# Placing every long SBUF row of an fp32 transformer kernel at a multiple of 512 bytes

## The chip, the cores and the metric

The kernel runs on one core of one Trainium2 chip. The metric is the device time of one execution in microseconds; the time quoted is the median of three runs.

## The reference

Two small models run one after the other on 256 tokens of 1,024 features, all in fp32. Block 1: a gated MLP mixer over 128-token blocks, a gated feed-forward layer with a causal convolution of width 3, attention over 64-token chunks with a relative bias, a second such feed-forward layer, and a norm. Block 2: a mixer that joins stick-breaking attention with a delta-rule recurrence, a feed-forward layer with a per-layer embedding gated in, latent attention with rotated keys, a second such layer, and the last norm. The products are the bulk of it; each has this form, `h` being 256 x K and `w` K x N:

```python
def conv_ffn(h, w_in, conv_w, conv_b, w_down):
    a = h @ w_in
    ...
    up, gate = jnp.split(a, 2, axis=-1)
    return (jax.nn.silu(gate) * up) @ w_down
```

## The kernel before

**The products.** Every weight matrix is cut into tiles of 128 x 128 and packed in the order of use, eight tiles to a chunk (`CT`), 399 chunks in all. `Net._chunk` (lines 392 to 406) loads a chunk of 128 x 1,024 fp32 into `raw` on SP's queue, ScalarE rounds it into a high part `whi` (line 404), and VectorE subtracts to get the low part `wlo` (line 405); both are of the type fp32r. Two chunks are prepared ahead of their use. The activations lie feature-major, 128 features by 256 tokens, and are cut the same way into `xh` and `xl` (`split`, lines 477 to 482). `gemm_tile` (lines 425 to 432) then makes three matmuls for each weight tile, each with a weight load of 128 columns and a moving operand of 256 columns:

```python
            self.mm(ps, wh, xh, start=first and k == 0, stop=False)
            self.mm(ps, wh, xl, start=False, stop=False)
            self.mm(ps, wl, xh, start=False, stop=k == n - 1)
```

`gemm_rows` (lines 450 to 460) turns the roles round for the attention values: the activations are the stationary operand and four weight tiles, 512 columns, move.

**The order.** In each phase TensorE takes its instructions as a list written by hand gives them (`GMLP_ORDER`, `ATT_ORDER`, `HYB_ORDER`, `MLA_ORDER`; `gated_layer`, lines 785 to 827, for the feed-forward layers). In `ffn1` (lines 829 to 869, the first block) both halves of the hidden row go through the convolution, in `ffn2` (lines 905 to 947) one does. Each has 22 hidden tiles, with 48 matmuls for the two halves of one (the up product), and then a product down of 8 output tiles with 66 matmuls each.

**The memory.** Each partition's SBUF is filled from both ends. From the low end, in `Net.__init__` (lines 328 to 334), come pools that live throughout: `cp` (gains and constants), `hp` (the residual rows `h`), `raw`, `whp`, `wlp`, `sp` (small and short tiles) and `xp` (operand tiles). The phases take turns at the two ends of what remains (`phase`, lines 463 to 469): a phase's pool holds its tiles, long and short ones mixed. A pool places each tag's buffers behind the last, in steps of 32 bytes. The kernel's first tile begins at byte 16,512; the gains (704 columns) and the first constants (258 columns) follow, so that `h` begins at byte 20,384, which is 416 past a multiple of 512. What lies behind keeps that offset until a short tile shifts it:

| tiles | begin, past a multiple of 512 | past a multiple of 64 |
|---|---|---|
| `h`, `raw`, `whi`, `wlo` | 416 | 32 |
| `xh`, `xl` of `xp`: most products | 224 | 32 |
| `xh`, `xl` of the mixer's and the attention's own pool | 480, 96 | 32 |
| `f1` tiles of the hybrid mixer, its last product | 288 | 32 |
| `hh`, `hl` (down products), `xh`, `xl` of the embedding's gate | 320 | 0 |
| `xh`, `xl` of the latent attention's own pool | 64 | 0 |

Every row of a tile, or of the slice that an instruction takes, is a multiple of 512 bytes here, so that the offset of a tile is that of all its slices: a weight tile's row is 512 bytes, a moving operand's 1,024 or 2,048.

**Short chains.** `newton` (lines 497 to 517) makes 1/sqrt for columns of 2, 4, 8 or 16 values per partition with eleven VectorE instructions, in tiles of that width.

Of the kernel before, what the change touches and what calls it, by code (L numbers as in the profile page):

```python
# [10 lines left out]
F32 = mybir.dt.float32  # L11
F32R = mybir.dt.float32r
I32 = mybir.dt.int32
# [7 lines left out]
P = 128  # L21
# [5 lines left out]
CT = 8           # 128x128 weight tiles in one chunk  # L27
HT = 2           # feature tiles of h in one load
LOOK = 2         # chunks prepared ahead of their use
# [5 lines left out]
# ---------------------------------------------------------------- layout tables  # L35
# per-feature vectors, one column of 128 values per feature tile
# [22 lines left out]
def _shape_consts():  # L59
    """Constants that depend on the shapes alone."""  # L60
# [28 lines left out]
    # rope: rows of a head's tile; even heads [64 plain | 32 cos | 32 sin], odd heads [32 sin | 32 cos | 64 plain]  # L89
# [24 lines left out]
# where, in steps of a gated layer's first product, what does not belong to it goes  # L114
# [40 lines left out]
class Sums:  # L155
    """sums of squares per token, gathered tile by tile"""
# [18 lines left out]
    def mean(self, dim):  # L175
        """mean of squares + eps, [128 tokens, 2]"""
        net = self.net
        ps = net.pa([P, 2])
        self.total(ps)
        x = net.t(net.sp, [P, 2], "msq")  # L180
        net.nc.vector.tensor_scalar(x, ps, 1.0 / dim, EPS, ALU.mult, ALU.add)
        return x


class Norm:
    """rms norm of h, gains applied: parts X of the unscaled rows at once, their scales in two later steps"""
# [22 lines left out]
class Last:  # L209
    """norm(h) * g of the last rows, gathered tile by tile, and its way out"""  # L210
# [15 lines left out]
    def total(self, n):  # L226
        """add up to n tiles"""
# [7 lines left out]
    def write(self):  # L235
# [5 lines left out]
        # 1/sqrt(x): square root and reciprocal, and a Newton step  # L241
        y, z, w, r = (net.t(net.sp, [P, 2], f"nwy2_{k}") for k in (0, 1, 2, 0))
# [17 lines left out]
class Hidden:  # L260
    """parts of a gated layer's hidden rows, each in three steps"""
# [25 lines left out]
class Embed:  # L287
    """half of norm(p @ w) * g, feature-major, in steps that go between the tiles of a longer product"""
# [31 lines left out]
class Net:  # L320
    def __init__(self, ctx, tc, d, nchunks):
# [5 lines left out]
        pool = lambda name, bufs, **k: ctx.enter_context(tc.tile_pool(name=name, bufs=bufs, **k))  # L327
        self.cp = pool("cp", 1)
        self.hp = pool("hp", 1)
# [16 lines left out]
    # ------------------------------------------------------------ small helpers  # L346
# [4 lines left out]
    def t(self, pool, shape, tag, dt=F32, **k):  # L351
        return pool.tile(shape, dt, tag=tag, name=self.uid(tag), **k)
# [20 lines left out]
    def load_consts(self, pool, group):  # L373
        w = sum(CONSTS[n].shape[1] for n in CGROUP[group])
        ct = self.t(pool, [P, w], "cst_" + group, bufs=1)
# [15 lines left out]
    # ------------------------------------------------------------ weights  # L391
# [16 lines left out]
    def after(self, ins):  # L408
        """VectorE issues this after the last chain of short operations"""
        if self.fence is not None:  # L410
            self.tc.add_manual_dep(ins.ins, self.fence.ins.name, NOSYNC, reason="order")

    def w(self, name, idx, k0, cols, n=1):
        """the next n 128x128 weight tiles, as (high, low) parts of [128, 128 n]"""
# [19 lines left out]
    def gemm_pair(self, X, ps, name, idx, parts, late=False, mid=None, at=0):  # L434
        """two output tiles in one bank; late: the last input tile comes last for both; mid: call within the second"""
# [10 lines left out]
    def pe_order(self):  # L446
        """TensorE takes its instructions as they are written down"""
        return self.tc.manual_schedule(engines={E.PE})

    def gemm_rows(self, X, ps2, name, idx, c0, ks=None, n=None, cols=lambda c0, j: ((c0 + j * P, P),)):  # L450
        """token-major: ps2[t] = tokens of block t by 512 columns"""
# [10 lines left out]
    # ------------------------------------------------------------ splits and norms  # L462
    @contextmanager
    def phase(self, name, xbufs=1):
        """a pool of its own for a phase; the phases take turns at the two ends of the free memory"""
        self.side ^= 1
        with self.tc.tile_pool(name=name, bufs=2, side="right" if self.side else "left", reuse_waits="tile") as p:
# [3 lines left out]
    def xtile(self, own=True):  # L471
        """high and low part of one operand tile, out of the phase's pool or of the one that all phases share"""
# [4 lines left out]
    def split(self, h, gain, own=True):  # L477
        """high and low parts of h * gain"""
# [18 lines left out]
    def newton(self, x, n, out=None, alone=False):  # L497
        """1/sqrt(x), x [128, n]"""
        v, sp = self.nc.vector, self.sp
        i = self.t(sp, [P, n], f"nwi{n}", I32)  # L500
        j = self.t(sp, [P, n], f"nwj{n}", I32)
# [3 lines left out]
        a = self.t(sp, [P, n], f"nwa{n}")  # L505
        b = self.t(sp, [P, n], f"nwb{n}")
        ys = [self.t(sp, [P, n], f"nwy{n}_{k}") for k in range(3)]
# [11 lines left out]
    def stats(self, tiles, dim):  # L519
        """rT [128 tokens, 2] = 1/rms, and the same along the free axis in every partition, [128, 256]"""  # L520
# [14 lines left out]
    def bcast(self, rT=None, dg=None):  # L535
        """[128 tokens, 2] -> along the free axis in every partition, [128, 256]"""
# [10 lines left out]
    def proj_residual(self, X, name, idx, tiles=range(KD), late=False):  # L547
        """late: the first two tiles take the last input tile at their ends"""
# [11 lines left out]
    # ------------------------------------------------------------ start  # L560
# [14 lines left out]
    # ------------------------------------------------------------ block 1  # L575
    def gmlp(self):
# [4 lines left out]
        with self.phase("gmlp", 8) as p:  # L581
# [49 lines left out]
            def mix(q):  # L631
                """two groups' values mixed over the tokens"""
# [20 lines left out]
    def out_steps(self, X, name, idx):  # L653
        """the steps of a product into h, each output tile in two, the second one for the last input tiles"""
# [12 lines left out]
    def steps(self, order, env):  # L667
        """a phase as a list of steps, name.argument.argument, in the order in which TensorE takes them"""
# [1042 lines left out]
```

## Time and profile before

| | |
|---|---|
| median of three runs | 1331.22 us (1328.53 to 1332.67) |
| profiled execution, span from first to last instruction | 1329.0 us |
| TensorE matmuls busy | 1302.5 us, 98% |
| weight loads busy | 1241.6 us, 93% |
| VectorE busy | 1026.6 us, 77% |
| ScalarE busy | 781.1 us, 59% |
| GpSimd busy | 15.7 us, 1% |
| TensorE's granted clock, mean of the span | 0.986 |

The profiled execution's own time is not listed apart from its span; the span lies 2.2 us under the median and inside the range of the three runs. Busy matmul time counts a matmul from its start to a modelled end, and neighbours overlap, so 98% says that TensorE always has a matmul under way, not that it runs at its best: for that one looks at the distance from one matmul's start to the next one's, the pitch.

### The profile page before, as it was taken

Reading aid. Unit: us, or ns where it says so; the run is one execution under the profiler, and the core shown is the slowest. Engines: PE = TensorE matmul, PEld = TensorE weight load, DVE = VectorE, ACT = ScalarE, POOL = GpSimd, SP = SyncE. Lnnn points to the kernel's source line nnn. Section 1 sums busy time; section 2 is a strip of 40 time slices with the busy share of each in tenths; the row PEclk is TensorE's granted clock in tenths of the full one; section 3 lists DMA queues with packets and bytes.
Section 4 is the critical chain, followed back from the end, with each engine's and each line's share of the span. In section 5 each row is a group of like instructions: output and inputs, shape, how many; then the busy total and the mean of one; then the engine's idle time right before and its main releaser. Section 6 shows DMA issues by size and latency. Waiting matters only on the chain.

```text
span 1329.0 us, 27117 instructions
## 1 busy us (share of the span) xinstructions
PE 1302.5 (98%) x10864; PEld 1241.6 (93%) x10864; DVE 1026.6 (77%) x2037; ACT 781.1 (59%) x1359; POOL 15.7 (1%) x48
## 2 busy tenths in 40 slices
PE   7999999999999999999999999999999999999997
PEld 5999999988899999999876799999998999999996
DVE  5889997666679997568964488887779978889655
ACT  6666665457667665448443265655556776565444
POOL 0000000000000000001100000000000000000000
PEclk9999999999999999999998799999999999999998
DMA  7565555555445555564440055555554335555551
GB/s 268 165 232 188 185 186 188 190 180 178 134 144 191 190 186 185 186 236 143 126 126 17 33 180 189 188 179 190 188 176 163 110 126 185 189 190 178 189 191 48
DMA packets 70397, 223.17 MB, mean 168 GB/s; under 512 B 13408, under 2 KB 15712, under 8 KB 70272
## 3 DMA queue, kind: packets, MB, share of 16 engines
q1 hardware_dynamic: 63312, 212.43, 47.9%
q10 hardware_dynamic: 6192, 5.34, 1.4%
q0 software_dynamic: 768, 3.67, 0.8%
q8 instruction: 85, 1.39, 0.4%
q14 instruction: 40, 0.33, 0.1%
HBM read 218.53 MB, written 2.88 MB: 167 GB/s over the span
## 4 chain that ended last, share of the span: by engine, by line
PE 94%; DVE 3%; DMA 1%; ACT 1%; issue 0%; SPq 0%; DVEq 0%; ACTq 0%
PE g L371 80%; PE s L371 6%; PE t L371 4%; PE o L371 3%; PE t L768 1%; DVE wlo L405 1%; DMA raw<-in_wall 1%; DMA b<-dZ 0%; DVE tm L1202 0%; DMA b<-dY 0%; DVE tm L1204 0%; DVE xl L481 0%; DMA dY<-tm 0%; DVE sqa L167 0%; ACT whi L404 0%
## 5 line engine op out<-in xcount | busy, mean ns | idle before, releaser
L371 PE MATMUL g<-xh,whi 128*128 128x256 f32 x2184 | 619.7, 284 | 1.4 <-ACT xh L480 1.4
L404 ACT ACTIVATE whi<-raw 128x1024 fp32r<-128x1024 f32 (+1 forms) x400 | 421.7, 1055 | 331.4 <-PE g L371 174.9
L405 DVE TENSOR_TENSOR wlo<-raw,whi 128x1024 fp32r<-128x1024 f32 (+1 forms) x400 | 487.4, 1220 | 166.8 <-ACT whi L404 165.6
L371 PE MATMUL g<-xl,whi 128*128 128x256 f32 x2184 | 611.6, 280 | 1.8 <-DVE xl L481 1.8
L371 PE MATMUL g<-xh,wlo 128*128 128x256 f32 x2184 | 610.5, 280 | 0.1
L371 PEld LDWEIGHTS g<-xh,whi 128*128 128x128 f32 x2184 | 411.3, 188 | 7.2 <-issue 4.0
L371 PEld LDWEIGHTS g<-xl,whi 128*128 128x128 f32 x2184 | 410.6, 188 | 3.1 <-DVE xl L481 2.4
L371 PEld LDWEIGHTS g<-xh,wlo 128*128 128x128 f32 x2184 | 410.5, 188 | 0.3 <-DVE wlo L405 0.3
L371 PE MATMUL g<-hl,whi 128*128 128x256 f32 x704 | 196.9, 280 | 0.0
L371 PE MATMUL g<-hh,whi 128*128 128x256 f32 x704 | 196.9, 280 | 0.0
L371 PE MATMUL g<-hh,wlo 128*128 128x256 f32 x704 | 196.9, 280 | 0.0
L371 PEld LDWEIGHTS g<-hh,wlo 128*128 128x128 f32 x704 | 132.3, 188 | 0.0
L371 PEld LDWEIGHTS g<-hh,whi 128*128 128x128 f32 x704 | 132.3, 188 | 0.0
L371 PEld LDWEIGHTS g<-hl,whi 128*128 128x128 f32 x704 | 132.3, 188 | 0.0
L273 ACT ACTIVATE hh<-pr 128x256 fp32r<-128x256 f32 x88 | 36.0, 409 | 49.4 <-DVE pr L268 49.4
L852 ACT ACTIVATE c<-pad,vec 128x256 f32<-128x256 f32 x88 | 47.7, 589 | 9.3 <-DVE pad L841 9.3
L480 ACT ACTIVATE xh<-h,vec 128x256 fp32r<-128x256 f32 x80 | 39.0, 498 | 23.9 <-DVE h L545 20.8
L859 DVE SCALAR_TENSOR_TENSOR c<-pad,vec,c 128x256 f32<-128x256 f32 x88 | 42.7, 485 | 3.1
L481 DVE SCALAR_TENSOR_TENSOR xl<-h,vec,xh 128x256 fp32r<-128x256 f32 x80 | 37.7, 478 | 6.8 <-ACT xh L480 6.8
L857 DVE SCALAR_TENSOR_TENSOR c<-pad,vec,c 128x256 f32<-128x256 f32 x88 | 42.1, 478 | 0.0
L278 DVE TENSOR_TENSOR hl<-pr,hh 128x256 fp32r<-128x256 f32 x88 | 36.8, 418 | 3.9 <-ACT hh L273 3.9
L371 PE MATMUL g<-whi,xh 128*128 128x512 f32 x68 | 29.4, 432 | 9.4 <-ACT xh L480 9.4
(375 smaller groups left out, 1392.8 us busy)
## 6 DMA issues: line engine op xcount, KB each, us to landing
raw<-in_wall SPq DMA_DIRECT2D x398, 512.0 KB, 3.5
bias<-in_bias POOLq DMA_DIRECT2D x4, 768.0 KB, 6.7
cst_c<-in_c ACTq DMA_DIRECT2D x1, 896.0 KB, 7.0
raw<-in_wall SPq DMA_DIRECT2D x2, 256.0 KB, 4.2
h<-in_x ACTq DMA_DIRECT2D x2, 256.0 KB, 4.4
h<-in_x POOLq DMA_DIRECT2D x2, 256.0 KB, 7.5
ws<-in_ws ACTq DMA_DIRECT2D x1, 512.0 KB, 8.5
bs<-in_bs ACTq DMA_DIRECT2D x1, 512.0 KB, 8.4
```

Of the source, the lines that this page charges most:

```text
L273: self.net.nc.scalar.activation(self.H[-1][0], self.pr, AF.Copy)
L278: self.net.nc.vector.tensor_tensor(hl, self.pr, hh.bitcast(F32), ALU.subtract)
L371: self.nc.tensor.matmul(out, lhsT=lhsT, rhs=rhs, start=start, stop=stop, skip_group_check=True)
L404: nc.scalar.activation(hi[:, s], raw[:, s], AF.Copy)
L405: self.after(nc.vector.tensor_tensor(lo[:, s], raw[:, s], hi[:, s].bitcast(F32), ALU.subtract))
L480: self.nc.scalar.activation(xh, h, AF.Copy, scale=gain)
L481: self.nc.vector.scalar_tensor_tensor(xl, h, gain, xh.bitcast(F32), ALU.mult, ALU.subtract)
L768: self.nc.tensor.transpose(pt[:, b * P:b * P + P], w[:, s * P:s * P + P], self.cst["ident"])
L852: a.activation(c0, pad[:, j, 2:], AF.Identity, bias=self.col("f_conv_b", (l,), j * KF + i), scale=cw(2, j))
L857: v.scalar_tensor_tensor(c1, pad[:, j, 1:S + 1], cw(1, j), cc[n], ALU.mult, ALU.add)
L859: v.scalar_tensor_tensor(cc[n], pad[:, j, 0:S], cw(0, j), c1, ALU.mult, ALU.add)
```

## The change

Comments are dropped, and these edits are made:

- Two tiles that nothing uses are placed, 672 bytes at the low end behind `cp` and a new pool `sp_odd`, and 480 bytes at the high end. With them `h` begins at byte 22,528 (44 x 512), and the tiles at the high end are placed down from byte 228,864 (447 x 512).
- `Net.t` sends a tile of `sp` or of a phase whose row isn't a whole multiple of 128 elements to a second pool (`sp_odd`, or the phase's name with `_odd`), opened inside the phase's own.
- Constants loaded for a phase get a tile rounded up to 128 columns.
- `newton` for 2, 4 and 8 columns uses tiles of 8 columns under one set of tags, of which it takes the first `n`; the last norm's `write` does the same.

No instruction's operation, shape or order in the source is changed. The core of the diff:

```diff
+ROW = 128
+LEFT_GAP, RIGHT_GAP = 672, 480
...
         self.cp = pool("cp", 1)
+        self.odd = {"sp": pool("sp_odd", 2)}
+        for side, n in (("left", LEFT_GAP), ("right", RIGHT_GAP)):
+            pool("gap_" + side, 1, side=side).tile([P, n // 4], F32, tag="gap", name=self.uid("gap"))
         self.hp = pool("hp", 1)
...
     def t(self, pool, shape, tag, dt=F32, **k):
+        if math.prod(shape[1:]) % ROW:
+            pool = self.odd.get(pool.name, pool)
         return pool.tile(shape, dt, tag=tag, name=self.uid(tag), **k)
...
-        ct = self.t(pool, [P, w], "cst_" + group, bufs=1)
+        ct = self.t(pool, [P, w if pool is self.cp else -(-w // ROW) * ROW], "cst_" + group, bufs=1)[:, 0:w]
...
         self.side ^= 1
-        with self.tc.tile_pool(name=name, bufs=2, side="right" if self.side else "left", reuse_waits="tile") as p:
+        pool = lambda n: self.tc.tile_pool(name=n, bufs=2, side="right" if self.side else "left", reuse_waits="tile")
+        with pool(name) as p, pool(name + "_odd") as odd:
+            self.odd[name] = odd
             self.p, self.xbufs = p, xbufs
             yield p
...
-        i = self.t(sp, [P, n], f"nwi{n}", I32)
-        j = self.t(sp, [P, n], f"nwj{n}", I32)
+        new = lambda tag, dt=F32: self.t(sp, [P, max(n, 8)], f"nw{tag}{max(n, 8)}", dt)[:, 0:n]
+        i, j = new("i", I32), new("j", I32)
...
-        a = self.t(sp, [P, n], f"nwa{n}")
-        b = self.t(sp, [P, n], f"nwb{n}")
-        ys = [self.t(sp, [P, n], f"nwy{n}_{k}") for k in range(3)]
+        a, b = new("a"), new("b")
+        ys = [new(f"y{k}_") for k in range(3)]
```

## Rows read from the trace of the kernel before

**Rows 1.** The page: span, TensorE's busy time, and the chain by engine and line.

```profile
span 1329.0 us, 27117 instructions
...
PE 1302.5 (98%) x10864; PEld 1241.6 (93%) x10864; DVE 1026.6 (77%) x2037; ACT 781.1 (59%) x1359; POOL 15.7 (1%) x48
...
PE 94%; DVE 3%; DMA 1%; ACT 1%; issue 0%; SPq 0%; DVEq 0%; ACTq 0%
```

**Rows 2.** Matmul groups by form: names, shapes, count | busy us, mean ns | idle before.

```profile
L371 PE MATMUL g<-xh,whi 128*128 128x256 f32 x2184 | 619.7, 284 | 1.4 <-ACT xh L480 1.4
...
L371 PE MATMUL g<-hh,whi 128*128 128x256 f32 x704 | 196.9, 280 | 0.0
...
L371 PE MATMUL g<-whi,xh 128*128 128x512 f32 x68 | 29.4, 432 | 9.4 <-ACT xh L480 9.4
...
L371 PE MATMUL g<-f,whi 128*128 128x256 f32 x128 | 23.8, 286 | 0.2 <-DVE f L494 0.2
...
L371 PE MATMUL s<-whi,xh 128*128 128x512 f32 x18 | 7.4, 411 | 0.0
```

**Rows 3.** Stretches: width, busy PE, PEld, DVE, ACT, POOL (instructions), clock, DMA, GB/s.

```profile
100.00:200.00 100.00, 100.00 (x851) 100.00 (x851) 97.55 (x164) 67.08 (x108) 0.00 (x0) 1.00 0.57 188
210.00:270.00 60.00, 60.00 (x513) 60.00 (x513) 36.84 (x51) 30.00 (x41) 0.00 (x0) 1.00 0.57 187
...
405.00:505.00 100.00, 100.00 (x851) 100.00 (x851) 97.54 (x163) 67.26 (x109) 0.00 (x0) 1.00 0.57 190
...
643.00:755.00 112.00, 108.91 (x1077) 81.38 (x1076) 64.72 (x163) 42.31 (x86) 0.12 (x2) 0.89 0.26 72
...
800.00:900.00 100.00, 100.00 (x850) 99.95 (x849) 84.81 (x146) 60.75 (x100) 0.00 (x0) 1.00 0.56 185
...
1030.00:1080.00 50.00, 50.00 (x397) 44.05 (x396) 40.38 (x144) 39.84 (x114) 0.00 (x0) 1.00 0.31 101
```

**Rows 4.** Timeline of TensorE, a key product of the attention: ten starts apart.

```profile
303.78 0.28 PE L371 MATMUL g<-xh,whi 128*128 128x256 f32 x1
...
304.96 0.28 PE L371 MATMUL g<-xl,whi 128*128 128x256 f32 x1
```

**Rows 5.** Timeline of TensorE, a query product of the attention: ten starts apart.

```profile
293.56 0.28 PE L371 MATMUL g<-xh,wlo 128*128 128x256 f32 x1
...
294.69 0.28 PE L371 MATMUL g<-xh,whi 128*128 128x256 f32 x1
```

**Rows 6.** Timeline of TensorE, the hybrid mixer's last product: nine starts apart.

```profile
772.82 0.40 PE L371 MATMUL g<-f,whi 128*128 128x256 f32 x2
...
773.90 0.40 PE L371 MATMUL g<-f,whi 128*128 128x256 f32 x2
```

**Rows 7.** Timeline of TensorE, a product down: twelve starts apart.

```profile
229.76 0.28 PE L371 MATMUL g<-hh,wlo 128*128 128x256 f32 x1
...
231.17 0.28 PE L371 MATMUL g<-hh,wlo 128*128 128x256 f32 x1
```

**Rows 8.** Timeline of TensorE, values of the attention, 512 columns: five starts apart.

```profile
300.27 0.39 PE L371 MATMUL s<-whi,xh 128*128 128x512 f32 x1
...
301.44 0.40 PE L371 MATMUL t<-wlo,xh 128*128 128x512 f32 x1
```

**Rows 9.** VectorE's groups by form: a chunk's low part, a step of `newton`.

```profile
L405 DVE TENSOR_TENSOR wlo<-raw,whi 128x1024 fp32r<-128x1024 f32 x398 | 486.1, 1222 | 160.9 <-ACT whi L404 159.7
...
L512 DVE TENSOR_TENSOR nwb<-nwa,msq 128x2 f32<-128x2 f32 x39 | 6.2, 160 | 1.1
```

**Rows 10.** TensorE's waits at the start of the hybrid mixer: us in total, times, longest.

```profile
PE g L371 <- ACT xh L480: 1.4, 1, 1.4
PE g L371 <- DVE xl L481: 0.9, 1, 0.9
```

**Rows 11.** The weight queue: packets, MB, share of 16 engines' span.

```profile
q1 hardware_dynamic: 63312, 212.43, 47.9%
```

More of the change, by code (lines that the diff above doesn't have):

```diff
@@ L240, in write @@
         v.tensor_scalar(x, self.ps, 1.0 / D, EPS, ALU.mult, ALU.add)
-        y, z, w, r = (net.t(net.sp, [P, 2], f"nwy2_{k}") for k in (0, 1, 2, 0))
+        y, z, w, r = (net.t(net.sp, [P, 8], f"nwy{k}_8")[:, 0:2] for k in (0, 1, 2, 0))
         net.nc.scalar.activation(y, x, AF.Sqrt)
```

## The prediction

> **What bounds the kernel now.** I read the page's busy shares and its chain of waits first [rows 1]. TensorE is busy for 1302.5 of 1329.0 us and carries 94% of the chain that sets the end; everything else there is 6%. So only TensorE's pitch can move the time much. The groups by form [rows 2] say where that pitch is paid: products with 256 moving columns. Each of the names xh,whi, xl,whi and xh,wlo has 2184 matmuls, the three of the hidden rows 704 each, the hybrid mixer's last product 128 + 64, and the embedding's product 96 (8 output tiles x 2 input tiles x 3, in two layers): 6552 + 2112 + 192 + 96 = 8952. With 512 columns there are 68 + 18 + 18, each three times: 312.
>
> Next I read the stretches [rows 3]. From 100 to 200 us, in an up product, 851 matmuls start or are under way; the first one has begun up to 0.28 us before, so the pitch is 100.28 / 851 = 117.8 ns. The same comes out at 405 to 505 us, and a down product has 60.28 / 513 = 117.5. The granted clock is 1.00 there, the 2.4 GHz level, at which 256 columns at one per cycle would be 106.7 ns. Some 11 ns of each matmul are therefore not its columns. The timeline tells more: ten starts of a key product take 1.18 us [rows 4], ten of a query product 9 us earlier 1.13 us [rows 5], nine of the hybrid's last product 1.08 us [rows 6], twelve of a down product 1.41 us [rows 7]. That is 118, 113, 120.0 and 117.5 ns for one shape at one clock. Neither traffic nor another engine need explain it: such a pitch holds for a whole product, and that of the up product is the same in the next layer.
>
> **A reading of these pitches.** I measure them in steps of 16 columns: 64 bytes of each partition, 6.67 ns at 2.4 GHz. They are 17.7, 17.0, 18.0 and 17.6 steps. Before the change a moving row of 1,024 bytes that begins 32 past a multiple of 64 touches 17 blocks of 64, and the weight tile's 512 bytes, always 32 past, touch 9. The best pitch seen for such rows is 17.0 steps, as if each block took one and nothing was lost; the usual one loses two thirds of a step more. Down products, whose moving rows begin at a multiple of 64 (16 blocks), still take 17.6 and are not seen at 17.0: there it would be the weights' ninth block that doesn't fit. This is inferred from four rates, not shown: no operand pair of these products begins at multiples of 64 on both sides.
>
> **The change, part by part.**
>
> *Operands of the products.* Both sides now begin at multiples of 512: 16 and 8 blocks. I take one step off the usual pitch, 117.8 - 6.7 = 111.1 ns, and the same 111.1 for the down products (from 117.5, so 6.4 off). The bounds: 106.7 (all stall gone), and above, 120.0, the worst that the trace shows [rows 6]. By the Trainium skill, "TensorE: Matmul & The Clock Gate", section "Back-to-back issue gap", a warm matmul needs N/2.4 + 2.5 ns, so 109.2 for 256 columns; the sum would then be some 12 us lower than mine. No row shows it.
>
> What of it reaches the end, stage by stage:
> - Up products of the second block, 2 x 22 x 48 = 2112 matmuls: VectorE is busy 84.81 of 100 us [rows 3]; those 100 us would shrink to 94.3, so it still fits. 2112 x 6.7 = 14.2 us.
> - Up products of the first block, also 2112: VectorE is busy 97.55 of 100 us there, so it becomes the bound. Of some 226 us in the two layers (112 and 114) at most 2.5% goes: 5.6 us, not 14.2. What is late next is the low part of a chunk (1222 ns each [rows 9]), two per hidden tile.
> - Down products, 2112: VectorE 36.84 of 60 us, ScalarE 30.00. 2112 x 6.4 = 13.5 us.
> - The rest, 8952 - 6336 = 2616 matmuls: 17.5 us, of which I count three quarters, 13 us, because in the attentions they stand between chains of VectorE and ScalarE (40.38 and 39.84 of 50 us in one [rows 3]).
> - 512 columns: pitch 1.17 / 5 = 234 ns [rows 8], 35 steps where 33 blocks are touched. One step off: 312 x 6.7 = 2 us.
>
> Sum: 14.2 + 5.6 + 13.5 + 13 + 2 = 48 us.
>
> *VectorE, ScalarE, DMA.* Their instructions read the same bytes from other places. I cost that at nothing: the up products of both blocks run the same low part in 1222 ns on average whatever surrounds it. The weight queue's packets fill 47.9% of the DMA engines' time [rows 11]; a few per cent either way stay hidden while 512 KB per chunk arrive ahead of 24 matmuls. If products run 6% faster the stretch's DMA share rises from 0.57 to about 0.60, still cover.
>
> *Short tiles.* `newton` issues the same eleven instructions of about 160 ns [rows 9] on the same slices; wider tiles change no duration. Calls with 2, 4 and 8 columns now share two buffers; writer and last reader are mostly VectorE in its own order, so a wait costs nothing, and at worst one link of 0.16 us in a few places.
>
> *Moved addresses between phases.* Tiles of a new phase overlap other tiles of the last ones, so a first writer can wait for another reader. Where it is a load, what is queued behind it waits too: ScalarE's rounding behind the constants, the bias behind GpSimd's fills, and the weight chunks on SP's queue behind the embedding's input and the zeroing of the blocks in DRAM (lines 293, 1034). For the last, two chunks prepared ahead are a cover of some 5.6 us (24 matmuls each at 117.8 ns). The nearest rows are the waits at the start of the hybrid mixer, 1.4 + 0.9 us [rows 10]. Seven phase changes at 0 to 2.3 us give -2 to +5 us (some waits may go); I take 0, because TensorE's first products of most phases read the shared pool, which has no such wait.
>
> The profiled execution has only its span: 1329.0 - 48 = 1281.0 us. The median lies 2.2 us above the span, which I keep: 1283 us.
>
> **Rivals.**
>
> *A. Faster by another amount.* If 17.0 steps are a floor that the hand-over from weight load to matmul sets, the pitch is 113.3: (2112 x 4.5 + 2112 x 4.2) ns = 18.4, plus 5.6, plus 3/4 of 2616 x 4.5 = 8.8, plus 1 to 2: 34 us, 1297 us. If all stall goes, 11.1 and 10.8 ns are saved where I counted 6.7 and 6.4: 46 + 5.6 + 22 + 6 = 80 us, 1251 us. For the first speaks that weight loads are busy 100 of 100 us; for the second nothing but the column count.
>
> *B. Nothing changes.* Rows that begin 96, 224 and 480 past 512 all have 117.8 as their usual pitch, and those at multiples of 64 lose just 0.3 ns of it; 113 and 118 occur with the same offsets in one phase. The layout itself does what is said: 20,384 + 1,472 bytes of short tiles + 672 = 22,528, and 229,344 - 480 = 228,864. But the offset may not be the cause, and what is left is how each product's first matmul falls against its weight load. Then the time is 1331, within -2 to +5 us. The Trainium skill, "SBUF — State Buffer", section "Specifications (TRN2)", gives lines of 16 bytes; every offset is a multiple of 32 already, so by that rule the change would do nothing. The near-equal pitch of 117.5 and 117.8 agrees with it; the 113 and 120 it doesn't explain.
>
> *C. Slower.* With one common offset each moving row and each weight row begin at the same phase, so their reads could meet in every matmul rather than in some. The place is the steady product, the price the 18.0 steps that the hybrid's last product already pays, where moving parts and weights hold one relation throughout: +2.2 ns x 6840 + 2.5 ns x 2112 = 20 us, 1351 us; there VectorE gives no relief, because TensorE is the bound. It decides as soon as the pitch of the up products exceeds 117.8. For it: rows at multiples of 64 never reach 113 [rows 7]. Against: reads that meet once per matmul should shift past each other after the first.
>
> **How the numbers follow.** My forecast, a pitch near 111, has a chance of 0.36; A's two ends together 0.27 (0.16 for 113, 0.11 for below 109); B 0.20; C 0.17. A run tells a difference from 0.3%, 4 us. So faster is 0.36 + 0.27 = 0.63, same 0.20, slower 0.17. The likeliest time is 1283, its own range 1270 to 1297. For 8 in 10 the range must take in A and B: from 1250 to 1336; it leaves out C and a little below.
>
> **What would show it.** Right: the same stretches with about 111 ns per matmul, the up products of the first block at 114 to 115 with VectorE at 99%, and TensorE there waiting on the low part. The stretch from 643 to 755 us, small matmuls with the granted clock at 0.89 [rows 3], keeps its length to 2 us. Wrong: the pitch at 117.8 with the same mix of 113 and 118 (B), or 120 in the up products (C). If DMA or VectorE durations change by over 2%, the alignment acts elsewhere than I looked. New waits over 2 us at a phase's start would show the moved addresses.

## The result and the profile after

The change makes the kernel slower: 1345.71 us median of four runs (1344.33 to 1349.52) beside 1331.95 us (1328.53 to 1336.1) for the kernel before in the same comparison, a ratio of 1.0111 with a 95% interval of 1.008 to 1.0143. The profiled execution took 1345.76 us with a span of 1344.0 us, 15.0 us more than before. The forecast was 1283 us, and its range ended at 1336.

First the page of the kernel after (span, busy times, the weight queue, the chain by engine), which answers to [rows 1, 11]:

```profile
span 1344.0 us, 27125 instructions
...
PE 1319.3 (98%) x10864; PEld 1260.2 (94%) x10864; DVE 1028.5 (77%) x2037; ACT 781.1 (58%) x1359; POOL 16.1 (1%) x48
...
q1 hardware_dynamic: 63312, 212.43, 47.5%
...
PE 93%; DVE 4%; DMA 2%; ACT 0%; issue 0%; SPq 0%; ACTq 0%; DVEq 0%
```

Of the 15.0 us, matmuls' busy time has 16.8; VectorE, ScalarE and the queue are where they were. So the time is in TensorE's own pace. The matmul groups by form (names, shapes, count | busy us, mean ns | idle before), the kernel after, beside [rows 2]:

```profile
L379 PE MATMUL g<-xh,whi 128*128 128x256 f32 x2184 | 626.5, 287 | 1.4 <-ACT xh L490 1.4
...
L379 PE MATMUL g<-hh,whi 128*128 128x256 f32 x704 | 199.2, 283 | 0.0
...
L379 PE MATMUL g<-whi,xh 128*128 128x512 f32 x68 | 28.9, 425 | 9.2 <-ACT xh L490 9.2
...
L379 PE MATMUL g<-f,whi 128*128 128x256 f32 x128 | 23.8, 287 | 0.2 <-DVE f L504 0.2
```

Products of 256 columns have grown, those of 512 have shrunk (432 to 425 ns), and the hybrid's last product stays: its pitch was 120.0 ns before [rows 6]. Stretches of the kernel after (width, busy time and count of PE, PEld, DVE, ACT, POOL, clock, DMA share, GB/s), moved by the delay so that they hold the same work as in [rows 3]:

```profile
100.00:200.00 100.00, 100.00 (x836) 100.00 (x835) 95.99 (x161) 65.54 (x106) 0.00 (x0) 1.00 0.56 185
213.00:273.00 60.00, 60.00 (x502) 60.00 (x502) 35.51 (x49) 28.65 (x39) 0.00 (x0) 1.00 0.55 182
405.00:505.00 100.00, 100.00 (x836) 100.00 (x835) 96.22 (x161) 66.73 (x109) 0.00 (x0) 1.00 0.56 186
...
805.00:905.00 100.00, 100.00 (x835) 99.95 (x834) 83.11 (x142) 59.42 (x99) 0.00 (x0) 1.00 0.55 184
```

At the same granted clock of 1.00, the 2.4 GHz level, 835 or 836 matmuls instead of 850 or 851 fit in 100 us. The pitch is 100.28 / 836 = 120.0 ns in the up products of both blocks (117.8 before) and 60.28 / 502 = 120.1 in the down products (117.5 before). VectorE's busy time per stretch falls with it (97.55 to 95.99 in the first).

Last the timeline (start us, us, engine, line, operation), of the attention's value product with 512 columns and of the query product behind it, which answer to [rows 8] and [rows 5]:

```profile
294.68 0.39 PE L379 MATMUL s<-whi,xh 128*128 128x512 f32 x1
...
295.81 0.39 PE L379 MATMUL t<-wlo,xh 128*128 128x512 f32 x1
...
297.11 0.28 PE L379 MATMUL g<-xh,whi 128*128 128x256 f32 x1
...
298.31 0.28 PE L379 MATMUL g<-xl,whi 128*128 128x256 f32 x1
```

Five starts of 512 columns take 1.13 us, 226 ns each (234 before); ten starts of the query product take 1.20 us, 120 ns each, where 113 ns was seen before. In all phases a product settles at the same 120.0, 18 steps of 6.67 ns; only the first ten matmuls of some attention products are a little quicker, at 118 to 119.

The starts of the same matmuls in both traces show that the loss grows with the products and nowhere jumps:

| from, to (start of a product) | before, us | after, us | difference |
|---|---|---|---|
| up, first block, first layer: 107.7 to 209.5 | 101.8 | 103.7 | +1.9 |
| up, first block, second layer: 400.2 to 513.3 | 113.1 | 115.2 | +2.1 |
| up, second block, first layer: 799.5 to 913.5 | 113.9 | 116.1 | +2.1 |
| up, second block, second layer: 1090.2 to 1228.3 | 138.1 | 140.7 | +2.6 |
| product down, first to last of its 528 matmuls, in each of the four layers | 61.8 | 63.2 | +1.4 |
| small matmuls of the hybrid mixer: 676.4 to 754.3 | 77.9 | 76.6 | -1.3 |

The up products sum to 8.8 us, the down products to 5.6, and 0.6 us is left for all the rest. That rest holds, besides the hybrid's 1.3, a beginning (to 20 us) that is 1.1 us shorter and an end behind the last matmul that is 0.8 shorter.

### The profile page after: what moved, and what is told of

Its sections match the earlier page's. It is cut to its first block, busy times and chain, and to the rows that moved or that the text cites. A ratio compares the mean times of both kernels' runs of the same rounds, so it can differ in the third digit from the quotient of the medians.

```text
span 1344.0 us, 27125 instructions
## 1 busy us (share of the span) xinstructions
PE 1319.3 (98%) x10864; PEld 1260.2 (94%) x10864; DVE 1028.5 (77%) x2037; ACT 781.1 (58%) x1359; POOL 16.1 (1%) x48
## 4 chain that ended last, share of the span: by engine, by line
PE 93%; DVE 4%; DMA 2%; ACT 0%; issue 0%; SPq 0%; ACTq 0%; DVEq 0%
PE g L379 80%; PE s L379 5%; PE t L379 3%; PE o L379 3%; PE t L777 1%; DVE wlo L413 1%; DMA raw<-in_wall 0%; DMA b<-dZ 0%; DVE tm L1211 0%; DMA tm<-dA 0%; DVE tm L1213 0%; DMA dA<-b 0%; DVE xl L491 0%; DMA b<-dY 0%; DMA dY<-tm 0%
## 5 line engine op out<-in xcount | busy, mean ns | idle before, releaser
L379 PE MATMUL g<-xh,whi 128*128 128x256 f32 x2184 | 626.5, 287 | 1.4 <-ACT xh L490 1.4
L379 PE MATMUL g<-xl,whi 128*128 128x256 f32 x2184 | 618.8, 283 | 1.7 <-DVE xl L491 1.7
L379 PE MATMUL g<-xh,wlo 128*128 128x256 f32 x2184 | 618.6, 283 | 0.0
L379 PEld LDWEIGHTS g<-xh,whi 128*128 128x128 f32 x2184 | 419.4, 192 | 7.0 <-issue 4.0
L379 PEld LDWEIGHTS g<-xl,whi 128*128 128x128 f32 x2184 | 419.5, 192 | 2.9 <-DVE xl L491 2.1
L379 PEld LDWEIGHTS g<-xh,wlo 128*128 128x128 f32 x2184 | 419.4, 192 | 0.2 <-DVE wlo L413 0.2
L379 PEld LDWEIGHTS g<-hh,whi 128*128 128x128 f32 x704 | 135.2, 192 | 0.0
L379 PEld LDWEIGHTS g<-hl,whi 128*128 128x128 f32 x704 | 135.2, 192 | 0.0
L379 PEld LDWEIGHTS g<-hh,wlo 128*128 128x128 f32 x704 | 135.2, 192 | 0.0
```

The costliest lines, as they stand in the source:

```text
L379: self.nc.tensor.matmul(out, lhsT=lhsT, rhs=rhs, start=start, stop=stop, skip_group_check=True)
```

## The experiments

Write **distance** for how far the weight row's start lies behind the moving row's start, modulo 256 bytes. Before, the up products have 416 - 224 = 192, the down products 416 - 320 = 96, the hybrid's last product 416 - 288 = 128, the queries of the attention, whose moving rows lie in its own pool, 416 - 96 = 320, which is 64; its keys, from the shared pool, have 192 like the up products. After, every distance of these products is zero.

Three theories stood at the start: **R**, the distance decides; **A**, rows at multiples of 64 or 512 are slow in themselves; **H**, what came before a product decides (theories 1, 2 and 3 in the first expectation). Later **P** joined, that the pools of short tiles, the moved phases or the wider `newton` tiles cost the time.

### The pitch by itself, at chosen offsets (m1_offsets)

This kernel does nothing of the reference. It runs 56 groups of 48 matmuls in the products' order, all of them twice, on rows at chosen places, in one execution at a granted clock of 0.999:

```diff
+                for g, (xo, wo, n) in enumerate(GROUPS * 2):
...
+                    a, b = xo // 4, wo // 4
...
+                    for r in range(2):
+                        for k in range(8):
+                            ks = slice(a + k * step, a + k * step + n)
+                            ws = slice(b + k * P, b + k * P + P)
+                            for w_, x_ in ((wh, xh), (wh, xl), (wl, xh)):
+                                nc.tensor.matmul(ps[:, 0:n], lhsT=w_[:, ws], rhs=x_[:, ks], start=i == 0, stop=i == m - 1,
...
```

> This kernel computes nothing of the reference: it loads some rows, makes high and low parts, and runs 110 groups of 48 matmuls of the product's form (weights of 128 columns loaded for each, moving operand of 256 columns, fp32r), each group with its own offset of the moving rows and of the weight rows past a multiple of 512 bytes, and all groups a second time; a few groups have other numbers of columns. Every group starts after TensorE has stood still. Theory 1, the two rows' reads meet, and what counts is where one begins against the other: with both at 0 the pitch is 120.0 ns as in the changed kernel, equal offsets on both sides (16 and 16, 64 and 64, 256 and 256) give 120.0 too, and some unequal pair gives 113.3 or less. Theory 2, multiples of 64 are bad in themselves: (0, 0) and (64, 64) give 120.0, but (16, 16) and (32, 32) give less. Theory 3, offsets do nothing and only the way in which a product begins decides: the two passes over the same offsets differ as much as different offsets do. By either of the first two the moving length enters as 16 columns a step of 6.67 ns plus a constant: 2 steps at (0, 0), so 106.7 ns for 224 columns, 133.3 for 288, 146.7 for 320 and 226.7 for 512, unless the weight load itself sets a floor, which the groups with 192 and 224 columns would show as a pitch that no longer falls.

Timeline of that kernel: three groups of 256 columns, 38 starts each, with (moving, weights) at (0, 0), (0, 64) and (64, 64) past a multiple of 512:

```profile
391.91 0.28 PE L65 MATMUL g<-xh,wh 128*128 128x256 f32 x1
...
396.47 0.28 PE L65 MATMUL g<-xh,wl 128*128 128x256 f32 x1
...
527.69 0.28 PE L65 MATMUL g<-xh,wh 128*128 128x256 f32 x1
...
532.00 0.28 PE L65 MATMUL g<-xh,wl 128*128 128x256 f32 x1
...
604.96 0.28 PE L65 MATMUL g<-xh,wh 128*128 128x256 f32 x1
...
609.52 0.28 PE L65 MATMUL g<-xh,wl 128*128 128x256 f32 x1
```

They take 4.56, 4.31 and 4.56 us: 120.0, 113.4 and 120.0 ns. Moving both rows by 64 bytes changes nothing, moving one of them by 64 takes a full step off. All groups at multiples of 32, by distance (ns per matmul, from the starts in the steady part of each group, both passes):

| distance | 0 | 32 | 64 | 96 | 128 | 160 | 192 | 224 |
|---|---|---|---|---|---|---|---|---|
| pitch | 120.0 (seven groups) | 118.3 | 113.3 (four groups), 117.8 (one) | 117.3 to 117.4 (one of four groups 118.6 in the first pass) | 118.6 to 118.8 | 119.9 to 120.1 | 117.8 | 117.8 (one of two groups 116.8 in the first pass) |

This is R in the main. Equal offsets of 32, 64, 128 and 256 all give the 120.0 of the kernel after, so A falls. But a distance doesn't always have one pace. Two groups changed theirs from the first pass to the second, and at distance 64 the rows at (448, 0) took 117.8 in both passes where those at (192, 0) took 113.3. Two distances of the kernel before give its pitches: 192 gives 117.8 and 96 gives 117.3. The third doesn't: 128 gives 118.7 here, while the hybrid's last product showed 120.0 [rows 6]. Below multiples of 32 the picture is finer: with both at 16 the pitch was 118.4, not 120.0, and with the weights beginning 4 bytes before the moving rows, at distance 252, it was 123.3.

Two more readings. With 192 columns the pitch is 111.7 at distance 0 and at 32, and with 224 columns it is the same: there something else sets it. The Trainium skill, "TensorE: Matmul & The Clock Gate", section "LDWEIGHTS (loading the stationary operand)", puts a weight load at its columns divided by 1.2, so an estimate by it for 128 columns is 106.7 ns, which these 111.7 ns are near; that the load sets this floor isn't shown. With 512 columns distance 0 is the better one, 226.7 ns beside 233.3 at 32, as in the kernel itself.

### Does the beginning matter? (m2_history)

Also nothing of the reference: the same groups, some begun right behind six matmuls of another width, and some with high and low parts at places of their own.

```diff
+                    if pre:
...
+                        for i in range(6):
+                            nc.tensor.matmul(s[:, 0:pre], lhsT=wh[:, i * P:i * P + P], rhs=xh[:, i * P:i * P + pre], start=i == 0,
...
+                            for w_, wo, x_, xo in ((wh, wa, xh, xa), (wh, wa, xl, xb), (wl, wb, xh, xa)):
+                                nc.tensor.matmul(ps[:, 0:S], lhsT=w_[:, wo // 4 + k * P:wo // 4 + k * P + P],
...
```

> Computes nothing of the reference: groups of 48 matmuls of 256 columns (three per weight pair, as in the kernel's products), with the high and low moving parts and the high and low weights at chosen bytes past a multiple of 512, some groups begun behind six matmuls of 128 or 512 columns of another product. Theory R (the pitch follows from the distance between the moving row's start and the weight row's, modulo 256, and from little else): distance zero 120.0 ns in every group whatever came before, weights 64 bytes ahead of the moving row's multiple 113.3 ns after every kind of beginning. Theory H (the beginning of a product decides between 113 and 118 or 120, and the offsets only in part): the same offsets give different pitches behind 0, 128 and 512 columns, with 118 to 120 for weights at 64 in some of them. If the three kinds of matmul each count by their own pair, low weights alone at 64 give two thirds of 120.0 and one third of 113.3, 117.8 ns.

Distance zero gave 120.0 ns in all nine of its groups that came after the warm-up. Distance 64 gave 113.3 in 14 of 18 groups and 117.8 in the other four (two behind six matmuls of 32 or of 384 columns, two behind a pause). One group at 192 ran at 113.3 and one at 128 at 120.0, where the others had 117.8 and 118.6 to 118.8; so the 120.0 of [rows 6] is a pace that distance 128 can have. Both theories hold a part: the distance sets which paces can last, and the beginning of a product picks one of them. Low weights alone at 64 gave 117.8, as a mean over the kinds would, but so did sets where that mean is another: high weights at 64 with low at 0 should give 115.6 and gave 117.8. The kernel before fits: the attention's queries (64) ran at 113.3 in five of eight products and at 117.8 in three, its keys (192) at 117.8 in seven of eight.

### A map of distances (m3_map)

Nothing of the reference either; 315 groups, each distance behind three or four beginnings.

```diff
+B = (0, 64, 128, 192)
+GROUPS = [((0, 0, w, w), pre) for w in range(0, 256, 8) for pre in (0, 32, 160, 384)]
+GROUPS += [((0, x, w, v), pre) for x in B for w in B for v in B if (x, w) != (0, v) for pre in (0, 32, 384)]
+GROUPS += [((0, 0, 64, v), pre) for v in (160, 224) for pre in (0, 32, 384)]
```

> Computes nothing of the reference: groups of 36 matmuls of 256 columns at chosen distances, each distance behind three or four kinds of beginning. First part: weights 0 to 248 bytes past the moving row's multiple of 512, in steps of 8. Theory R (the distance alone sets the pitch): one pitch per distance, whatever the beginning; 113.3 ns in a narrow range around 64 bytes, 120.0 at zero. Theory R+H (the distance sets which pitches can hold, the beginning picks one): zero has 120.0 alone, 64 bytes has 113.3 and 117.8, and perhaps some distance has 113.3 alone. Second part: high and low parts at different multiples of 64. If each of the three kinds of matmul counted by its own pair only, the pitch would be the mean of the three pairs' pitches, and nothing with a pair at distance zero would go below 115.6 ns (two thirds of 113.3 and one third of 120.0); if the sequence counts, some mixed set holds 113.3 behind every beginning.

Timeline of that kernel, 21 starts of each of three groups, all with moving parts at 0: both weights at 64 behind a pause, the same behind matmuls of 160 columns, and high weights at 64 with low ones at 192 behind a pause:

```profile
197.84 0.28 PE L66 MATMUL g<-xl,wh 128*128 128x256 f32 x1
...
200.31 0.28 PE L66 MATMUL g<-xl,wh 128*128 128x256 f32 x1
...
208.58 0.28 PE L66 MATMUL g<-xl,wh 128*128 128x256 f32 x1
...
210.96 0.28 PE L66 MATMUL g<-xl,wh 128*128 128x256 f32 x1
...
806.83 0.28 PE L66 MATMUL g<-xl,wh 128*128 128x256 f32 x1
...
809.21 0.28 PE L66 MATMUL g<-xl,wh 128*128 128x256 f32 x1
```

2.47, 2.38 and 2.38 us: 117.6, 113.3 and 113.3 ns. What the map adds:

- Zero has 120.0 behind all four beginnings, but so have 112, 160 and 216 bytes. Both weights at 64 or at 192 now had 117.8 behind three beginnings and 113.3 behind one. The expected narrow range of 113.3 around 64 isn't there: 56 and 72 bytes gave 117.5 to 118.5, while 88 and 168 bytes reached 113.3 behind three of four beginnings.
- Of the sets with high and low parts apart, just one held 113.3 behind all three beginnings: moving parts at 0, high weights at 64, low weights at 192. The low weights' own pair alone has 117.8 as a rule, so the three kinds of matmul don't count each by itself; that their sequence counts is inferred.
- High weights at 64 with low at 160 gave 117.8 behind all three. That is the control for the kernel below.

### Distance zero at other places (all32) and in the kernel before (b_rel0)

```diff
-LEFT_GAP, RIGHT_GAP = 672, 480
+LEFT_GAP, RIGHT_GAP = 672 + 32, 480 - 32
```

> The kernel after, with every row of whole 512 bytes at 32 bytes past a multiple of 512: no operand of a product begins at a multiple of 64, and the distance between moving and weight rows is still zero. Theory R (the distance): 120.0 ns in all products of 256 columns, 1345 us, as after. Theory A (the multiples of 64 or 512 themselves are slow): back to about 117.8 ns and 1331 us. By the prediction's own reading, in which each block of 64 bytes that is touched costs a step, one block more for each side: 120.0 plus 6.7 to 13 ns, over 1390 us.

The other takes the kernel before and adds one gap ahead of the shared short tiles, so that the up products come to distance 0 and the down products to 416 - 0 = 160. Whatever lies behind the gap moves by its 192 bytes; nothing else of the change is in it:

```diff
         self.wlp = pool("wlp", 3)
+        pool("gap_x", 1).tile([P, 192 // 4], F32, tag="gap", name=self.uid("gap"))
         self.sp = pool("sp", 2)
```

> The kernel before with one gap of 192 bytes ahead of the shared short-tile pool, which moves the shared moving parts to 416 bytes past a multiple of 512, where the weights are, and the hidden rows from 320 to 0; pools of short tiles and the inverse square root stay as they were. Theory R: the up products go from 117.8 to 120.0 ns, 4224 x 2.2 ns = 9 us, and the down products, now 96 past the weights as in a group that took 119.9 ns, from 117.4 to 120, 5 us: about 1346 us. Theory A (multiples of 64 or 512): moving rows stay 32 past a multiple of 64 in the up products, so no change there, and 5 us at most from the down products, 1331 to 1337 us. Theory P (the pools of short tiles, the moved phase pools and the wider square root cost the time, not the products): no change, 1331 us.

Measured: 1347.67 us (ratio to before 1.0144, interval 1.011 to 1.0179) and 1344.7 us (1.0117, 1.0091 to 1.0143). Up products in a stretch of the first kernel:

```profile
100.00:200.00 100.00, 100.00 (x836) 100.00 (x835) 96.04 (x161) 65.30 (x106) 0.00 (x0) 1.00 0.57 185
```

Two of its products with 512 columns, ten starts apart:

```profile
285.02 0.39 PE L379 MATMUL g<-whi,xl 128*128 128x512 f32 x1
...
287.29 0.39 PE L379 MATMUL t<-wlo,xh 128*128 128x512 f32 x1
```

Up and down products in stretches of the second kernel:

```profile
100.00:200.00 100.00, 100.00 (x836) 100.00 (x835) 96.21 (x161) 65.29 (x105) 0.00 (x0) 1.00 0.59 185
213.00:273.00 60.00, 60.00 (x502) 60.00 (x502) 36.06 (x49) 28.85 (x41) 0.00 (x0) 1.00 0.56 184
```

836 in 100 us is 120.0 ns, 502 in 60 us is 120.1, the pace that distance 160 had by itself. In the first no operand of these products begins at a multiple of 64, and it is as slow as the kernel after: A falls a second time, and so does the prediction's reading, by which these rows would touch a block more on both sides. Its products with 512 columns take 2.27 us for ten, 227 ns each, as in the kernel after and not the 234 of the kernel before, though their rows straddle blocks as they did there. The second is the kernel before but for one gap, and it loses as much as the whole change: P isn't needed, and the control below shows that its parts cost nothing.

### Weights 64 bytes behind the moving rows (w64)

```diff
-LEFT_GAP, RIGHT_GAP = 672, 480
+LEFT_GAP, RIGHT_GAP = 672 - 448, 480
...
         self.wlp = pool("wlp", 3)
+        pool("gap_x", 1).tile([P, 448 // 4], F32, tag="gap", name=self.uid("gap"))
```

> The kernel after, with weights, h and raw chunks moved to 64 bytes past a multiple of 512 and every moving part left at a multiple of 512. Theory R (the distance between the two rows): products of 256 columns at 113.3 ns, those of 512 columns perhaps back at 233 ns; from the kernel before that is 9.4 us in the up products of the second block, 5.6 us in those of the first, where VectorE becomes the bound, 8.5 us in the down products and up to 8.7 us in the rest, so 1297 to 1302 us, faster than both kernels. Theory A (rows at multiples of 64 or 512 are slow in themselves, whatever the distance): weights and moving rows are still at multiples of 64, so 120 ns and 1345 us. Theory H (the beginning of each product decides): a mix of 113 and 118, some 1320 us.

1314.74 us, ratio 0.9885 (0.9861 to 0.9909): faster than both kernels, but short of R's 1297 to 1302. Stretches of this kernel: the mixer's products, up products of the first block and of the second, then the end of these with the down products behind them, and down products alone:

```profile
70.00:85.00 15.00, 15.00 (x135) 15.00 (x134) 13.68 (x25) 11.42 (x20) 1.11 (x4) 1.00 0.81 277
...
100.00:200.00 100.00, 100.00 (x851) 100.00 (x850) 97.57 (x163) 67.13 (x108) 0.00 (x0) 1.00 0.58 189
...
805.00:865.00 60.00, 60.00 (x512) 60.00 (x511) 48.66 (x77) 37.63 (x63) 0.00 (x0) 1.00 0.58 186
890.00:950.00 60.00, 60.00 (x532) 60.00 (x531) 48.57 (x85) 34.34 (x49) 0.00 (x0) 1.00 0.61 193
...
915.00:965.00 50.00, 50.00 (x443) 50.00 (x442) 35.54 (x61) 27.00 (x36) 0.00 (x0) 1.00 0.60 194
```

15.28 / 135 = 113.2 ns, 100.28 / 851 = 117.8, 60.28 / 512 = 117.7, 60.28 / 532 = 113.3, 50.28 / 443 = 113.5. So H's mix is what came, at both paces that this distance showed by itself. The timeline shows where the pace changes here: where short matmuls of other tiles slip in between.

```profile
86.30 0.50 PE L380 MATMUL s<-cst_c,sqa 128*128 128x1 f32 x4
...
883.98 0.59 PE L380 MATMUL t<-dg,cst_c 128*128 128x256 f32 x2
```

Up to the first of these the mixer's products run at 113.3, behind it all up and down products of the first block's first layer at 117.8. The second layer is at 117.8 too; in the attention between them the products change from one pace to the other. Behind the second interruption, within the up product of the second block's first layer, 117.8 gives way to 113.3, and the down products take that over.

### The set that holds one pace (w64_192) and its control (w64_160)

To the edit of w64 a gap between the two weight pools is added, and the last gap shrinks by as much:

```diff
+        pool("gap_w", 1).tile([P, 128 // 4], F32, tag="gap", name=self.uid("gap"))
         self.wlp = pool("wlp", 3)
-        pool("gap_x", 1).tile([P, 448 // 4], F32, tag="gap", name=self.uid("gap"))
+        pool("gap_x", 1).tile([P, 320 // 4], F32, tag="gap", name=self.uid("gap"))
```

> The kernel after, with moving parts left at multiples of 512, high weights 64 bytes past and low weights 192 bytes past one: the set that held 113.3 ns behind every beginning when measured by itself. Theory R+H (the distances set which pitches can hold, the beginning picks one): all products of 256 columns at 113.3 ns, where the kernel with both weights at 64 had 113.3 in some products and 117.8 in the rest. From the kernel before that is 9.4 us in the up products of the second block, 5.6 us in those of the first, where VectorE becomes the bound, 8.5 us in the down products and 5 to 8 us in the rest: 1297 to 1303 us. Theory V (what kept the kernel with both weights at 64 from 1300 us is VectorE or the transfers, not the pitch): no better than that kernel, 1315 us.

In the control the gaps are 96 and 352 bytes.

> As the other kernel of this call, but low weights at 160: the set measured by itself at 117.8 ns behind every beginning. Theory R+H: 117.8 ns in the products, 1328 to 1333 us, no different from before. If any set with high weights at 64 did it, 1300 to 1315 us; if the low part counted by itself, a mean of two thirds of 113.3 to 117.8 and one third of 120.0, 115.6 to 118.5 ns.

Measured: 1292.4 us, ratio 0.9734 (0.9703 to 0.9765), faster than both kernels by far; and the control 1328.22 us, ratio 1.0003 (0.9977 to 1.0029). 32 bytes of the low weights' place are worth 36 us. The page of the faster one:

```profile
span 1294.2 us, 27125 instructions
...
PE 1266.6 (98%) x10864; PEld 1206.5 (93%) x10864; DVE 1020.6 (79%) x2037; ACT 786.5 (61%) x1359; POOL 16.1 (1%) x48
```

Its stretches, up products of both blocks and down products:

```profile
100.00:200.00 100.00, 100.00 (x885) 100.00 (x884) 98.69 (x169) 71.13 (x111) 0.00 (x0) 1.00 0.62 195
805.00:905.00 100.00, 100.00 (x882) 99.95 (x881) 85.84 (x147) 60.78 (x97) 0.00 (x0) 1.00 0.60 192
206.00:256.00 50.00, 50.00 (x443) 50.00 (x443) 32.13 (x43) 25.13 (x36) 0.00 (x0) 1.00 0.62 199
```

The up products of the control:

```profile
100.00:200.00 100.00, 100.00 (x851) 100.00 (x851) 97.60 (x163) 67.58 (x109) 0.00 (x0) 1.00 0.59 190
```

The busy share of TensorE is 98% as in both kernels; only the pitch tells. 100.28 / 885 = 113.3 ns, 100.28 / 882 = 113.7 and 50.28 / 443 = 113.5, against 117.8 in the control. R+H gave 1297 to 1303 and came out some 5 us too slow; V falls. Here too other matmuls slip in: behind those at 774, 869 and 961 us eight starts follow that are 117 to 125 ns apart, and then the pace is 113.3 again. The control has the change's pools, phases and `newton` tiles and the pace of before, and takes the time of before (ratio 0.9977 to 1.0029): those parts cost nothing that shows.

## Why the prediction was wrong

**What bounds the kernel** was right: TensorE's pitch alone moves the time, and a step of 6.67 ns is its grain.

**The step that failed** is the first term of the change: "I take one step off the usual pitch, 117.8 - 6.7 = 111.1 ns". It rested on the reading that each touched block of 64 bytes costs a step, and that the weights' ninth block was what didn't fit. The runs show another cause: the pitch of 256 columns follows the place of the moving rows against the weight rows. Aligned rows at distance zero take 18.0 steps; so do rows that straddle blocks at distance zero; and 17.0 steps are reached by rows that touch 16 and 8 blocks (w64) and also by those of before that touch 17 and 9 [rows 5]. At distance zero the pitch of a steady product is 120.0 ns where 111.1 was forecast, so the term is a loss of 2.2 to 2.7 ns per matmul and not a gain of 6.4 to 6.7.

For 512 columns the forecast step came off, but by luck: all32 has it with rows that straddle blocks, so it is the distance there as well, not the alignment. Over all consecutive starts the mean went from 233.4 to 228.9 ns, worth some 312 x 4.5 ns = 1.4 us where 2 were counted.

**Rival C** named the condition, its place and its pitch: both sides at one phase, in every matmul, 120.0 ns. Its mechanism, that reads meet, fits but isn't shown. It got 0.17 because "reads that meet once per matmul should shift past each other after the first". Whatever costs the time, it doesn't pass: the 120.0 ns last through every product. The row that spoke for C, the hybrid's last product at a steady 120.0 [rows 6], was the best evidence at hand, and a product with one fixed relation of its rows deserved more weight than an argument from how reads ought to behave. There was luck in that row, too: its distance is 128, which by itself mostly gave 118.7. C's price was 20 us against 15.0 measured between the spans (13.8 between the medians): up products 9.3 counted, 8.8 found; down products 5.3 and 5.6; the rest 5.8 and 0.6. In the rest the 512-column products gave some 1.4 back, the small matmuls of the hybrid mixer 1.3, the beginning and the end 1.9, and the hybrid's 192 matmuls were at 120 already. The range ended at 1336 and left C out.

**Rival A** was the right floor under the wrong condition: 113.3 ns is the best pitch that a run of 256 columns showed here, and it comes from distances, not from alignment. Its 34 us are what w64_192 gained, a span shorter by 1329.0 - 1294.2 = 34.8 us, in part by chance, since 8.2 us came in the first block's up products where A had 5.6. The 109.2 ns that the prediction estimates from the Trainium skill ("TensorE: Matmul & The Clock Gate", section "Back-to-back issue gap") was reached by no product of 256 columns in these runs. The 12 us that it works out from them would have made its sum of gains larger, not lower.

**Rival B**, no change, falls with the first stretch. Its 113 and 118 "with the same offsets in one phase" were mostly queries and keys, which lie at distances 64 and 192. The rule named beside it, lines of 16 bytes (the Trainium skill, "SBUF — State Buffer", section "Specifications (TRN2)"), would make all these places equal as the prediction reads it. They are all multiples of 32 and differ by up to 6.7 ns per matmul, 113.3 to 120.0, so the measurement decides: the rule doesn't give the pace of these products.

**VectorE as the next bound** in the first block's up products isn't what happened where it could be seen. It was put at 97.55 of 100 us busy, so "at most 2.5%" was to be had. In w64_192 the two stages went from 101.8 to 97.9 us and from 113.1 to 108.8 (starts of the same products), 3.8% each, the whole gain in pitch. VectorE's groups in that kernel, from 100 to 200 us:

```profile
L415 DVE TENSOR_TENSOR wlo<-raw,whi 128x1024 fp32r<-128x1024 f32 x37 | 45.1, 1219 | 0.0
L870 DVE SCALAR_TENSOR_TENSOR c<-pad,vec,c 128x256 f32<-128x256 f32 x38 | 18.4, 485 | 1.4
L868 DVE SCALAR_TENSOR_TENSOR c<-pad,vec,c 128x256 f32<-128x256 f32 x37 | 17.7, 479 | 0.0
L852 DVE TENSOR_TENSOR pad<-g,rb 128x512 f32<-128x512 f32 x19 | 13.0, 684 | 0.0
L280 DVE TENSOR_TENSOR hl<-pr,hh 128x256 fp32r<-128x256 f32 x19 | 8.0, 418 | 0.0
L270 DVE TENSOR_TENSOR pr<-sg,c 128x256 f32<-128x256 f32 x19 | 7.9, 416 | 0.0
```

They sum to 110.1 us in a stretch where VectorE is busy 98.69: neighbours overlap. A busy share near 98% was then no measure of what was left.

**The terms at nothing** were right. The low part takes 1223 ns as against 1222, a step of `newton` 160 as before, and the waits at the hybrid mixer's start are those of [rows 9, 10] again. VectorE's groups by form of the kernel after:

```profile
L413 DVE TENSOR_TENSOR wlo<-raw,whi 128x1024 fp32r<-128x1024 f32 x398 | 486.4, 1223 | 168.4 <-ACT whi L412 165.9
...
L521 DVE TENSOR_TENSOR nwb<-nwa,msq 128x2 f32<-128x2 f32 x39 | 6.2, 160 | 1.1
```

Its waits of TensorE around 590 us:

```profile
PE g L379 <- ACT xh L490: 1.4, 1, 1.4
PE g L379 <- DVE xl L491: 0.9, 1, 0.9
```

## What to carry to other kernels

When TensorE streams weights and moving rows with hardly a gap, look at where the two rows begin against each other, not at how each is aligned: measure the pitch of a steady product at several distances in a small kernel, behind several beginnings, and place the pools by that. Making all offsets alike makes all distances zero, which at 120.0 ns was, with 160 bytes, the slowest of the multiples of 32 here. A pitch that differs between products of one shape at one clock is a sign that such a choice is open.

## What the runs showed of the hardware

- With three matmuls of 256 columns per pair of weight tiles, in the float32 form used here, the pitch at multiples of 32 bytes is 113.3 to 120.0 ns by the distance of the rows and, at some distances, by how the product begins: 6% of the time of most of this kernel's products. At distance zero it is 120.0 at every absolute offset of 0, 32, 64, 128 and 256.
- Distances 64 and 192 have two lasting paces, 113.3 and 117.8 ns. In w64 a pace lasts over hundreds of matmuls and over the border of two products, and changes where other matmuls come between: from 113.3 to 117.8 at 86 us, back at 884.
- High and low weights at 64 and 192 behind the moving rows held 113.3 behind every beginning tried.
- With 512 columns distance zero is the better one (226.7 against 233.3 ns, and 227 in all32 with no row at a multiple of 64), and with 192 or 224 columns 0 and 32 bytes give the same 111.7 ns.

Which part of the memory or of TensorE makes the two streams wait for each other was not separated: that their reads meet is an inference from the dependence on distance, and no run was made in which weights stay loaded. Nor is it settled why the set of 64 and 192 has one lasting pace alone, or what in a beginning picks the pace at 64.
